# A convolution buffer of its own, and modulation chunks moved out of the output projection

## The chip, the cores and the metric

The kernel runs on one core of a Trainium2 chip. The metric is the device time of one execution in microseconds (us); the profiled execution also has a span, from its first to its last instruction. Engines are named as in the profile: PE is TensorE (matmuls), PEld its weight loads, DVE is VectorE, ACT is ScalarE, POOL is GpSimd, SP is SyncE, which only issues DMAs here.

## The reference

Two layers of a diffusion backbone over 512 latent tokens and a prefix of 256 context tokens, width 2048. Each layer makes three modulation vectors from a conditioning vector, runs one input projection that feeds four groups, and one output projection:

```python
for l in range(DEPTH):                       # DEPTH = 2
    need_ctx = l < DEPTH - 1
    shift, scale, gate       = split(silu(c)     @ w_mod[l] + b_mod[l], 3)
    shift_c, scale_c, gate_c = split(silu(c_ctx) @ w_mod[l] + b_mod[l], 3)
    hl = rmsnorm(x,  g_pre[l]) * (1 + scale)   + shift
    hc = rmsnorm(xc, g_pre[l]) * (1 + scale_c) + shift_c
    pl, pc = split_proj(hl @ w_in[l]), split_proj(hc @ w_in[l])
    oA = chunk_sgu(p[0], p[1]) * silu(p[2])                 # spatial gating (SGU)
    oB = diff_attention(p[3..5]) * silu(p[6])
    oC = rwkv_mixer(p[7..9]) * silu(p[10])                  # both directions, a recurrence
    oD = short_conv(p[11], p[12], p[13]) * silu(p[14])      # three taps, bg * conv(cg * xin)
    x  = x  + gate   * rmsnorm(concat(oA..oD) @ w_out[l], g_post[l])
    if need_ctx: xc = xc + gate_c * rmsnorm(the same for the context, g_post[l])
return x
```

All of it is float32. Layer 1 needs the context only as keys, values and recurrent state.

## The kernel before

Activations stand transposed: 128 features by 768 tokens (256 context, then 512 latent). A projection tile (`mtile`, lines 281 to 306) is 128 output features: four steps, each with one 256 KB weight load on SP (`wr`), a rounding to a high part on ACT (`wh`, L276), a low part on POOL or, in every fourth step, on DVE (`wl`, L277), and 12 matmuls of 512 columns (latent), with 12 more of 256 where the context is wanted. The result is in a bank of PSUM from the pool `mm`, which has three; a tile with context takes two.

The stages follow each other in each layer:

- **Recurrence** (`recurrence`): for each of four feature tiles (ft) a chain over six segments of 256 tokens. A pipeline (`rwkv_pipe`) interleaves three segments: features (`seg_pre`), a triangular inverse (`seg_inverse`) and the chain (`seg_chain`), and then `seg_y`, which writes the segment's output into `yacc`. When ft is done, `rwkv_merge` normalises `yacc`, adds `bacc`, gates it and stores it (L888), beside the first segment of the next ft. Projection tiles of later ft (`rkv_tile`, `gate_tiles`) are issued between segments and fill PE. Behind the recurrence stand the convolutions that share its pool: two in layer 0, four in layer 1. A convolution (`conv`) is four projection tiles: `x`, the product `zp`, three taps into `o`, a product and a gate, a store (L1118).
- **Groups** (`groups_phase`): four attention heads, two convolutions among them in layer 0, then four SGU heads.
- **Output** (`out_mid` in layer 0): 16 projection tiles m for the latent tokens (v = 0), their normalisation, residual and the next layer's input; then the same for the context (v = 1). `out_last` is that of layer 1.

Buffers: a tag of a pool with `bufs=1` is one buffer. In the recurrence the tag `x` serves a temporary at the start, `bacc` of ft 0 and 2, and the convolution's `x`; the tag `o` serves a temporary at the start, `yacc` of ft 0 and 2, and the convolution's `o`; `bacc` and `yacc` have tags of their own for ft 1 and 3.

Modulation: the vector products are done in chunks (jobs) of 512 outputs. `gemv_dve` loads 16 slices of `w_mod` and adds them up on DVE, for both vectors (L222; the first product of each sum on ACT, L220); `gemv_end` sums over partitions with matmuls and adds the bias (L250, L253). Twelve jobs stand in layer 0's groups and output: four gates of layer 0 and eight chunks for layer 1. Eight run one beside each attention and SGU head, and four beside the 16 output tiles of v = 0, there in halves of 256 columns. Their instructions have lower priority than what is written around them.

The program's order on each engine, and on SP's queue, is fixed when it is built: a scheduler places every instruction by priority (program order, unless `high_priority` raises it) as soon as its inputs and its buffers allow it. On the chip each queue runs in that order.

Of the kernel before, what the change touches and what calls it, by code (L numbers as in the profile page):

```python
# [9 lines left out]
F32 = mybir.dt.float32  # L10
F32R = mybir.dt.float32r
F16 = mybir.dt.float16
AF = mybir.ActivationFunctionType
# [6 lines left out]
NCTX = 256  # L20
NLAT = 512
T = NCTX + NLAT
KT = 16
# [15 lines left out]
PADW = 774  # L39
# [64 lines left out]
class Kernel:  # L104
# [661 lines left out]
    def seg_y(self, s):  # L766
        l, ft, st, seg, want_y = (s[k] for k in ("l", "ft", "st", "seg", "want_y"))
        GM, SV, UV, AR = (s[k] for k in ("GM", "SV", "UV", "AR"))
        nc, rp, ps = self.nc, self.rp, self.ps
        V, A = nc.vector, nc.scalar  # L770
        if want_y:
            yp = ps.tile([128, 4, 2, 64], F32, tag="ps", name=self.nm("yp"))
            two = lambda t: t.rearrange("p a t -> p (a t)")
            for c in range(4):
                nc.tensor.matmul(out=yp[:, c], lhsT=two(UV[:, c]), rhs=GM[:, c, 1], start=True, stop=False)
                nc.tensor.matmul(out=yp[:, c], lhsT=two(SV[:, c]), rhs=AR[:, c, :, 1, :], start=False, stop=True)
            if "yacc" not in st:
                st["yacc"] = rp.tile([128, PADW], F32, tag=("o", "yacc")[ft % 2], name=self.nm("yacc"))
            ycol = st["yacc"][:, seg * SEG:(seg + 1) * SEG].rearrange("p (c t) -> p c t", c=4)
            for h in range(2):  # L780
                hs = slice(64 * h, 64 * h + 64)
                if st.get(("y", seg)):
                    V.tensor_tensor(out=ycol[hs], in0=yp[hs, :, h, :], in1=ycol[hs], op=ALU.add)
                else:
                    A.copy(out=ycol[hs], in_=yp[hs, :, h, :])
            st["y", seg] = True
# [104 lines left out]
    def groups_phase(self, l):  # L891
        nc, tc = self.nc, self.tc
        with tc.tile_pool(name=self.nm("gr"), bufs=1, reuse_waits="tile") as gp, \
                tc.tile_pool(name=self.nm("gsp"), bufs=3, space=PSUM, reuse_waits="tile") as sp, \
                tc.tile_pool(name=self.nm("gpp"), bufs=2, space=PSUM, reuse_waits="tile") as pp:
            self.gp, self.sp, self.pp = gp, sp, pp
            self.cs = gp.tile([128, 2, NLAT], F32, tag="cs", name=self.nm("cs"))
            nc.sync.dma_start(out=self.cs, in_=self.a["rope"])
            self.rot = gp.tile([128, 128], F32, tag="rot", name=self.nm("rot"))
            nc.sync.dma_start(out=self.rot, in_=self.a["rot"])  # L900
            self.sgw = gp.tile([128, 4, 128], F32, tag="sgw", name=self.nm("sgw"))
            nc.sync.dma_start(out=self.sgw, in_=self.a["sgw"][l])
            self.sgb = gp.tile([128, 4, 128], F32, tag="sgb", name=self.nm("sgb"))
            nc.sync.dma_start(out=self.sgb, in_=self.a["sgb"][l:l + 1].to_broadcast([128, 4, 128]))
            jobs = [(0, j, (0, 1)) for j in range(8, 12)] + [(1, j, (0, 1)) for j in range(8)]
            if l > 0:
                jobs = [(1, j, (0,)) for j in range(8, 12)]
            else:
                self.jobs, jobs = jobs[8:], jobs[:8]

            open_jobs = []
            late = ({('a', 1): 2, ('a', 3): 3}, {})[l]

            def mod_jobs(n):
                for ll, j, acc in open_jobs:
                    self.gemv_end(ll, j, acc, pp, "pp")
                open_jobs.clear()
                for _ in range(min(n, len(jobs))):
                    ll, j, vecs = jobs.pop(0)
                    with tc.high_priority(offset=-1000):  # L920
                        open_jobs.append((ll, j, self.gemv_dve(ll, j, vecs, gp, "gw", 4, ("gacc0", "gacc1"))))
            for h in range(4):
                mod_jobs(1)
                self.attention(l, h)
                if ("a", h) in late:
                    self.conv(l, late["a", h])
            for h in range(4):
                mod_jobs(1)
                self.sgu(l, h)
                if ("s", h) in late:  # L930
                    self.conv(l, late["s", h])
            mod_jobs(0)
# [156 lines left out]
    def conv(self, l, f):  # L1089
        nc, gp = self.nc, self.gp  # L1090
        V, G, A = nc.vector, nc.gpsimd, nc.scalar
        ctx = l < DEPTH - 1
        cs = slice(0 if ctx else NCTX, T)
        segs = ([(0, 0, NCTX, 2)] if ctx else []) + [(1, NCTX, NLAT, 260)]
        cw = self.P(l, "conv").rearrange("p (k f) -> p k f", k=3)
        x = gp.tile([128, T], F32, tag="x", name=self.nm("x"))
        p = self.proj(l, 6336 + f * 128, ctx=ctx)
        self.evac(x[:, 0:NCTX], x[:, NCTX:T], p)
        zp = gp.tile([128, PADW], F32, tag="stg" if gp is self.rp else "cz", bufs=2, name=self.nm("zp"))
        for c in (0, 258, 772):  # L1100
            G.memset(zp[:, c:c + 2], 0.0)
        p = self.proj(l, 6848 + f * 128, ctx=ctx)
        for i, o0, n, po in segs:
            with self.tc.high_priority():
                V.tensor_tensor(out=zp[:, po:po + n], in0=p[i][:, 0:n], in1=x[:, o0:o0 + n], op=ALU.mult)
        o = gp.tile([128, T], F32, tag="o", name=self.nm("o"))
        for i, o0, n, po in segs:
            s = slice(o0, o0 + n)
            A.activation(out=o[:, s], in_=zp[:, po:po + n], func=AF.Copy, scale=cw[:, 1, f:f + 1])
            for k, d in ((0, -1), (2, 1)):  # L1110
                V.scalar_tensor_tensor(out=o[:, s], in0=zp[:, po + d:po + d + n], scalar=cw[:, k, f:f + 1],
                                       in1=o[:, s], op0=ALU.mult, op1=ALU.add)
        p = self.proj(l, 5824 + f * 128, ctx=ctx)
        for i, o0, n, po in segs:
            V.tensor_tensor(out=o[:, o0:o0 + n], in0=p[i][:, 0:n], in1=o[:, o0:o0 + n], op=ALU.mult)
        sg = self.gate2(gp, self.proj(l, 7360 + f * 128, ctx=ctx), "stg" if gp is self.rp else "cz", 2)
        V.scalar_tensor_tensor(out=o[:, cs], in0=o[:, cs], scalar=0.5, in1=sg[:, cs], op0=ALU.mult, op1=ALU.mult)
        nc.sync.dma_start(out=self.od[12 + f][:, cs], in_=o[:, cs])  # L1118
# [13 lines left out]
    def out_mid(self, l):  # L1132
        nc, tc = self.nc, self.tc
        V, A = nc.vector, nc.scalar
        self.hc, self.hl = ([], []), ([], [])
        with tc.tile_pool(name=self.nm("op"), bufs=2, reuse_waits="tile") as op, \
                tc.tile_pool(name=self.nm("ops"), bufs=1, space=PSUM, reuse_waits="tile") as ops:
            for v in (0, 1):
                n = (NLAT, NCTX)[v]
                ts = slice(NCTX, T) if v == 0 else slice(0, NCTX)  # L1140
                y = [op.tile([128, n], F32, tag=f"y{v}", bufs=KT, name=self.nm("y")) for _ in range(KT)]
                pre = [self.wload(self.a["w_out"][l, :, 0], 128, (1 + i) % 4) for i in range(4)]
                self.wraw = op, 4
                o = self.load_o(v)
                accs, open_jobs = [], []
                for m in range(KT):
                    if v == 0 and m % 4 == 1:
                        for job in open_jobs:
                            self.gemv_end(*job, ops, "rs")
                        open_jobs = []  # L1150
                        if self.jobs:
                            ll, j, vecs = self.jobs.pop(0)
                            with tc.high_priority(offset=-1000):
                                acc = self.gemv_dve(ll, j, vecs, op, "y1", KT, ("y1", "y1"), NCTX, KT)
                            open_jobs.append((ll, j, acc))
                    p = self.mtile(self.a["w_out"][l, :, m], 128, o if v else None, None if v else o, 1,
                                   pre=None if m else pre)[1 - v]
                    sq = op.tile([128, n], F32, tag=f"acc{m}{v}" if m < 2 else f"sq{v}", bufs=1, name=self.nm("sq"))
                    A.activation(out=sq, in_=p[:, 0:n], func=AF.Square)
                    A.copy(out=y[m], in_=p[:, 0:n])  # L1160
                    if m < 2:
                        accs.append(sq)
                    else:
                        V.tensor_tensor(out=accs[m % 2], in0=accs[m % 2], in1=sq, op=ALU.add)
                for job in open_jobs:
                    self.gemv_end(*job, ops, "rs")
                rs = self.rstd_bcast(op, ops, "rs", accs, n, f"rs{v}")
                acc2 = []
                for m in range(KT):
# [13 lines left out]
                rs = self.rstd_bcast(op, ops, "rs", acc2, n, f"rs{v}")  # L1183
# [109 lines left out]
```

## Time and profile before

| | us |
|---|---|
| median of three runs | 3751.13 (3750.08 to 3751.83) |
| the profiled execution | 3740.13 |
| its span | 3738.3 |
| PE busy | 3448.6 (92%) |
| DVE busy | 2303.8 (62%) |
| ACT busy | 1863.0 (50%) |
| POOL busy | 1364.5 (36%) |

Busy time is a sum over the whole span, and a matmul's end is modelled, so that PE at 92% says only that most of the span has matmuls in it. The stages have different limits, and the rows below are taken by stage.

### The profile page before, as it was taken

How to read it: one execution, taken by the hardware profiler on the slowest of the kernel's cores; microseconds unless marked ns; L12 is line 12 of the kernel's file. 1: busy time of each engine (PE TensorE's matmuls, PEld its weight loads, DVE VectorE, ACT ScalarE, POOL GpSimd, SP SyncE). 2: the span in 40 equal slices, each digit the busy share in tenths (PEclk: the TensorE clock that was granted, in tenths of full speed). 3: DMA queues.
4: the chain of work that ended last, by engine and by line, in shares of the span. 5: the costliest groups of instructions: out<-in, count | busy, mean ns of one | idle time of the engine just before them, and what ended most of it. 6: DMA issues, size and time to landing. Idle time of an engine off the chain costs nothing. (4 is left out here: it accounts for less than half of the span.)

```text
span 3738.3 us, 61946 instructions
## 1 busy us (share of the span) xinstructions
PE 3448.6 (92%) x22388; PEld 2811.2 (75%) x22388; DVE 2303.8 (62%) x4659; ACT 1863.0 (50%) x4131; POOL 1364.5 (36%) x1729
## 2 busy tenths in 40 slices
PE   7999999989999999999897899999778999999998
PEld 2477777767877888888676777777566787788798
DVE  5856777777386546463878734767667526643354
ACT  4466666766244344223324435767666524544454
POOL 2244444534222222222444433545334332322343
PEclk9999999989999999999999999999668999999999
DMA  8432222211343313344655433122011244423565
GB/s 306 183 116 65 59 66 67 60 48 38 104 130 96 112 51 95 112 139 134 201 156 184 123 115 89 56 69 60 28 29 46 60 133 132 139 71 85 166 188 179
DMA packets 239747, 400.90 MB, mean 107 GB/s; under 512 B 25936, under 2 KB 95568, under 8 KB 235344
## 3 DMA queue, kind: packets, MB, share of 16 engines
q1 hardware_dynamic: 232528, 386.45, 34.3%
q10 hardware_dynamic: 6912, 10.49, 0.8%
q8 instruction: 176, 2.88, 0.3%
q14 instruction: 131, 1.07, 0.1%
HBM read 363.28 MB, written 33.56 MB: 106 GB/s over the span
## 5 line engine op out<-in xcount | busy, mean ns | idle before, releaser
L306 PE MATMUL p<-h,wh 128*128 128x512 f32 (+3 forms) x8576 | 2160.1, 349 | 34.5 <-ACT y L1160 10.7
L306 PEld LDWEIGHTS p<-h,wh 128*128 128x128 f32 (+1 forms) x8576 | 1415.4, 190 | 236.1 <-ACT h L276 15.8
L306 PE MATMUL p<-h,wl 128*128 128x512 f32 (+2 forms) x4288 | 1344.5, 350 | 46.1 <-DVE wl L277 28.9
L277 POOL TENSOR_TENSOR wl<-wr,wh 128x512 fp32r<-128x512 f32 (+1 forms) x535 | 768.4, 1439 | 1501.7 <-ACT wh L276 1317.8
L276 ACT CAST wh<-wr 128x512 fp32r<-128x512 f32 (+1 forms) x756 | 465.8, 617 | 974.1 <-PE p L306 772.2
L306 PEld LDWEIGHTS p<-h,wl 128*128 128x128 f32 (+1 forms) x4288 | 748.4, 190 | 147.7 <-DVE wl L277 35.8
L222 DVE SCALAR_TENSOR_TENSOR acc<-gw,sil,acc 128x512 f32<-128x512 f32 (+1 forms) x636 | 458.5, 778 | 27.4 <-DMA gw<-in_w_mod 25.1
L277 DVE TENSOR_TENSOR wl<-wr,wh 128x512 fp32r<-128x512 f32 (+1 forms) x221 | 160.9, 728 | 218.6 <-ACT wh L276 216.8
L804 PEld LDWEIGHTS <-ib 128*128 128x128 f16 x2304 | 133.2, 103 | 138.1 <-issue 70.0
L839 ACT CAST ib<-xa 64x256 f16<-64x256 f32 x480 | 176.2, 367 | 18.0 <-PE xa L809 12.2
L829 DVE TENSOR_TENSOR T<-inv,c 128x256 f16<-128x256 f32 x240 | 98.9, 412 | 34.5 <-PE inv L804 31.4
L1001 DVE TENSOR_REDUCE sm<-s 128x1 f32<-128x256 f32 (+1 forms) x144 | 74.8, 538 | 73.5 <-PE s L999 72.3
L741 POOL TENSOR_SCALAR sp<-SV,pcs 64x64 f32<-64x64 f32 x160 | 80.8, 509 | 105.5 <-DVE SV L762 81.0
L652 POOL TENSOR_TENSOR bk<-t_tw,kr 64x256 f32<-64x256 f32 x96 | 92.9, 968 | 36.1 <-DVE kr L636 32.4
L745 PE MATMUL ch<-SV,GM 128*128 128x128 f32 x384 | 89.5, 317 | 17.5 <-DVE SV L762 10.1
L1008 ACT ACTIVATE e<-s,sm 128x256 f32<-128x256 f32 (+1 forms) x144 | 80.9, 569 | 41.6 <-DVE sm L1005 33.3
L706 PE MATMUL g<-AR,BK 128*128 128x256 f32 (+1 forms) x384 | 96.7, 391 | 3.9 <-DVE BK L658 1.9
L748 PE MATMUL ch<-zs,xb 128*128 128x64 f32 x384 | 81.3, 296 | 15.0 <-ACT zs L747 13.6
L748 PEld LDWEIGHTS ch<-zs,xb 128*128 128x128 f32 x384 | 65.7, 204 | 38.5 <-ACT zs L747 32.5
L753 PE MATMUL ch<-UV,BKT 128*128 128x128 f32 x352 | 85.6, 328 | 9.6 <-ACT UV L750 8.6
L762 DVE SCALAR_TENSOR_TENSOR SV<-ch,pcs,sp 64x64 f32<-64x64 f32 x256 | 72.1, 281 | 35.4 <-PE ch L753 28.2
L745 PEld LDWEIGHTS ch<-SV,GM 128*128 128x128 f32 x384 | 64.4, 204 | 37.6 <-issue 9.3
(270 smaller groups left out, 5022.0 us busy)
## 6 DMA issues: line engine op xcount, KB each, us to landing
wr<-in_w_in SPq DMA_DIRECT2D x484, 256.0 KB, 2.7
wr<-in_w_out SPq DMA_DIRECT2D x256, 256.0 KB, 2.9
gw<-in_w_mod SPq DMA_DIRECT2D x192, 256.0 KB, 3.0
gw<-in_w_mod SPq DMA_DIRECT2D x32, 1024.0 KB, 6.6
gw<-in_w_mod SPq DMA_DIRECT2D x128, 128.0 KB, 3.2
raw<-rkvd SPq DMA_DIRECT2D x96, 128.5 KB, 2.2
lz<-lzd SPq DMA_DIRECT2D x48, 256.0 KB, 3.1
os<-od SPq DMA_DIRECT2D x32, 256.0 KB, 3.2
```

What stands on the lines that cost most here:

```text
L222: self.nc.vector.scalar_tensor_tensor(out=acc, in0=w, scalar=s, in1=acc, op0=ALU.mult, op1=ALU.add)
L276: self.nc.scalar.copy(out=hi, in_=raw)
L277: eng.tensor_tensor(out=lo, in0=raw, in1=hi, op=ALU.subtract)
L306: nc.tensor.matmul(out=p[0:w, 0:n], lhsT=a[:, kk, :], rhs=x[b][k], start=(first and kk == 0 and i == 0), stop=(last and kk == 3 and i == 2))
L652: G.tensor_tensor(out=bk[hs, :, h, :], in0=c4(an)[hs], in1=kn[hs], op=ALU.mult)
L706: nc.tensor.matmul(out=g[:, c], lhsT=bkc(c2 + c), rhs=AR[:, c2 + c, :, 0:nk, :], start=True, stop=True)
L745: nc.tensor.matmul(out=chp[:, 0:128], lhsT=two(GM[:, c, 0]), rhs=two(SV[:, c]), start=True, stop=True)
L748: nc.tensor.matmul(out=chp[:, 128:192], lhsT=XT32[:, c, :], rhs=zs, start=True, stop=True)
L753: nc.tensor.matmul(out=chp[:, 192:320], lhsT=BKT[:, c, :], rhs=two(UV[:, c]), start=True, stop=True)
L804: nc.tensor.matmul(out=out[:, c, :], lhsT=lhsT[:, c, :], rhs=rhs(c), **kw(c))
L829: V.tensor_tensor(out=T1, in0=p1, in1=bt(self.lm(d, j)), op=ALU.mult)
L839: A.copy(out=half(XT, h), in_=aXT[hs])
```

## The change

Three things. In the recurrence every ft's `yacc` has one tag and buffer of its own, `yacc`; the convolutions there use the tag `o` for `x` and write `o` into the same buffer, so that they share nothing with `yacc` and `bacc`. The four modulation jobs beside the output tiles move to the SGU heads of layer 0, which get two jobs each, in whole slices of 512 columns. And the two ACT copies out of each output tile's PSUM get high priority.

```diff
@@ seg_y
-                st["yacc"] = rp.tile([128, PADW], F32, tag=("o", "yacc")[ft % 2], name=self.nm("yacc"))
+                st["yacc"] = rp.tile([128, PADW], F32, tag="yacc", name=self.nm("yacc"))
@@ groups_phase
-                self.jobs, jobs = jobs[8:], jobs[:8]
+                self.jobs = []
...
             for h in range(4):
-                mod_jobs(1)
+                mod_jobs(1 if l else 2)
                 self.sgu(l, h)
@@ conv
-        x = gp.tile([128, T], F32, tag="x", name=self.nm("x"))
+        own = gp is self.rp
+        x = gp.tile([128, PADW if own else T], F32, tag="o" if own else "x", name=self.nm("x"))
...
-        o = gp.tile([128, T], F32, tag="o", name=self.nm("o"))
+        o = x if own else gp.tile([128, T], F32, tag="o", name=self.nm("o"))
@@ out_mid
-                accs, open_jobs = [], []
+                accs = []
                 for m in range(KT):
-                    if v == 0 and m % 4 == 1:
-                        for job in open_jobs:
-                            self.gemv_end(*job, ops, "rs")
-                        open_jobs = []
-                        if self.jobs:
-                            ll, j, vecs = self.jobs.pop(0)
-                            with tc.high_priority(offset=-1000):
-                                acc = self.gemv_dve(ll, j, vecs, op, "y1", KT, ("y1", "y1"), NCTX, KT)
-                            open_jobs.append((ll, j, acc))
                     p = self.mtile(self.a["w_out"][l, :, m], 128, o if v else None, None if v else o, 1,
                                    pre=None if m else pre)[1 - v]
                     sq = op.tile([128, n], F32, tag=f"acc{m}{v}" if m < 2 else f"sq{v}", bufs=1, name=self.nm("sq"))
-                    A.activation(out=sq, in_=p[:, 0:n], func=AF.Square)
-                    A.copy(out=y[m], in_=p[:, 0:n])
+                    with tc.high_priority():
+                        A.activation(out=sq, in_=p[:, 0:n], func=AF.Square)
+                        A.copy(out=y[m], in_=p[:, 0:n])
...
-                for job in open_jobs:
-                    self.gemv_end(*job, ops, "rs")
```

## Rows read from the trace of the kernel before

**Rows 1.** Part 1 of the profile page: busy time by engine.
```profile
PE 3448.6 (92%) x22388; PEld 2811.2 (75%) x22388; DVE 2303.8 (62%) x4659; ACT 1863.0 (50%) x4131; POOL 1364.5 (36%) x1729
```

**Rows 2.** Stretches: length, busy PE PEld DVE ACT POOL, PE clock, DMA share, GB/s.
```profile
1000.00:1100.00 100.00, 95.12 (x530) 80.37 (x529) 76.58 (x116) 32.87 (x65) 33.64 (x22) 0.98 0.54 165
1500.00:1768.00 268.00, 258.78 (x1497) 225.49 (x1495) 132.48 (x258) 77.10 (x133) 58.60 (x42) 0.99 0.42 125
1768.00:1969.00 201.00, 177.29 (x786) 143.69 (x786) 146.15 (x284) 61.91 (x114) 96.59 (x48) 0.98 0.59 178
1800.00:1925.00 125.00, 103.74 (x456) 83.13 (x456) 120.17 (x238) 35.20 (x66) 68.14 (x27) 0.99 0.62 189
1969.00:2107.00 138.00, 111.28 (x785) 100.94 (x784) 114.97 (x131) 66.94 (x132) 69.63 (x49) 0.94 0.54 168
```

**Rows 3.** Stretches, projection matmuls (L306) alone: length, PE, PEld, clock, DMA, GB/s.
```profile
795.00:820.00 25.00, 0.00 (x0) 0.00 (x0) 0.58 0.08 22
820.00:964.00 144.00, 90.73 (x400) 61.27 (x401) 0.99 0.18 50
964.00:1009.00 45.00, 45.00 (x258) 39.13 (x257) 1.00 0.26 73
2610.00:2830.00 220.00, 0.00 (x0) 0.00 (x0) 0.67 0.09 26
2830.00:2985.00 155.00, 89.37 (x291) 50.58 (x292) 0.96 0.20 55
2985.00:3063.00 78.00, 78.00 (x346) 64.59 (x345) 1.00 0.37 105
```

**Rows 4.** Instructions in order of time, 2836 to 2842 us.
```profile
2837.95 0.72 POOL L884 TENSOR_TENSOR yacc<-yacc,bacc 128x256 f32<-128x256 f32 x1
2838.70 0.59 ACT L333 COPY x<-p 128x512 f32<-128x512 f32 x1 [0.75 <-POOL yacc L884]
...
2839.16 0.33 SPq L888 DMA_DIRECT2D od<-yacc  x1
```

**Rows 5.** Instructions in order of time: a write of `yacc`, and its stores.
```profile
471.32 0.75 ACT L785 COPY yacc<-yp 64x256 f32<-64x256 f32 x2 [0.65 <-PE yp L776]
...
475.68 0.32 SPq L888 DMA_DIRECT2D od<-yacc  x1
...
826.51 0.32 SPq L888 DMA_DIRECT2D od<-yacc  x1
...
2670.96 0.33 SPq L888 DMA_DIRECT2D od<-yacc  x1
...
2984.28 0.33 SPq L888 DMA_DIRECT2D od<-yacc  x1
```

**Rows 6.** One line of the kernel, L888: its DMAs from issue to landing.
```profile
DMA to landing us min/median/max: 2.0/2.3/3.3
```

**Rows 7.** Groups by form, 1500 to 1768 us: busy, mean ns, idle before.
```profile
L222 DVE SCALAR_TENSOR_TENSOR acc<-gw,sil,acc 128x512 f32<-128x512 f32 x90 | 74.0, 879 | 0.0
L277 POOL TENSOR_TENSOR wl<-wr,wh 128x512 fp32r<-128x512 f32 x42 | 58.6, 1395 | 207.7 <-ACT wh L276 207.7
```

**Rows 8.** Groups by form, 1768 to 1969 us.
```profile
L222 DVE SCALAR_TENSOR_TENSOR acc<-gw,sil,acc 128x256 f32<-128x256 f32 x240 | 123.2, 584 | 8.8 <-DMA gw<-in_w_mod 8.8
L277 POOL TENSOR_TENSOR wl<-wr,wh 128x512 fp32r<-128x512 f32 x48 | 97.0, 2028 | 112.5 <-ACT wh L276 104.1 <-DMA gw<-in_w_mod 8.4
L306 PE MATMUL p<-h,wl 128*128 128x512 f32 x241 | 96.3, 399 | 21.4 <-DVE wl L277 14.1 <-POOL wl L277 7.1
```

**Rows 9.** Waits: total us, times, longest; DVE's from 1500 to 1768.
```profile
DVE mod L253 <- PE gps L250: 53.0, 4, 13.4
```

**Rows 10.** Waits of PE from 1969 to 2107.
```profile
PE p L306 <- ACT y L1160: 10.7, 1, 10.7
```

**Rows 11.** Waits of SP's queue from 1500 to 2120.
```profile
SPq L236 <- DVE acc L222: 66.9, 98, 3.0
```

## The prediction

> **What bounds the kernel now.** I read busy time first [rows 1]: PE is the engine that sets the pace over the whole, so a change pays where PE stands idle or is out of work, and costs where it makes PE wait. Next come the stretches by stage [rows 2], and then the same with the projection matmuls alone [rows 3], because only these can be moved about; the rest of PE's work in the recurrence waits for its own chain. Two stretches of the recurrences hold no projection at all: 25 us in layer 0 (795 to 820) and 220 us in layer 1 (2610 to 2830). In the second PE's granted clock averages 0.67, so two thirds of it ran at the lower of the two levels. Right behind each recurrence stands the opposite: 45 us (964 to 1009) and 78 us (2985 to 3063) in which PE does projections alone. These are convolutions that came too late. What held them is seen in order of time [rows 4]: `x` of the first convolution is copied out of PSUM at the moment in which the merge of ft 2 has read `bacc` for the last time, at 2838.7. The buffer was the limit, not the priority.
>
> In the output stage [rows 2] PE is idle for 201 - 177.3 = 23.7 us of v = 0, where DVE is 96% busy from 1800 to 1925, and PE waits for low parts `wl` from DVE and POOL [rows 8]. Of v = 1 one wait of 10.7 us stands out, for a copy of ACT out of PSUM [rows 10].
>
> **The convolutions of layer 1.** They need no less work, but may now run from the start of the recurrence. The place for them is the empty 220 us. Beside the chain, the kernel before hosts 291 projection matmuls in the 155 us from 2830 on [rows 3], 1.88 per us. The empty stretch could so take 413; what is left over at 2985 is 346. All of it fits, by a margin of 67. The recurrence itself should not get longer: a feature tile takes (826.51 - 475.68) / 2 = 175 us in layer 0 with PE full, the empty one in layer 1 takes 2839.16 - 2670.96 = 168, and the last one, with convolutions beside it, 145 [rows 4, 5]. So the stage ends with the last merge at 2984.3, not with the last convolution at 3063: at most 79 us. I take 75, for a small hole at the turn to the groups; if hosting is a fifth slower (330 matmuls), 16 stay behind, and with a slower chain 60 is my lower bound.
>
> At full PE the higher clock comes back too, but the row of 168 us against 175 says that the chain gains nothing from it, so I count it as zero. The Trainium skill (TensorE: Matmul & The Clock Gate, Terms) prices time at a lowered clock at that time times the share of pulses withheld; that would give a further gain, which is a rival below. No run here has yet shown the chain faster for it.
>
> **The convolutions of layer 0.** The empty 25 us take 25 x 400 / 144 = 69 matmuls, and at the end 258 of them took 45 us: 12 us. PE is nearly full before that, so I expect little more. Bounds: 0, and 25 if the narrow gaps ahead of 795 are filled as well.
>
> **One buffer for `x` and `o`.** The next convolution's `x` now waits for the store of the one before, 2.0 to 3.3 us by the same kind of store [rows 6]; two projection tiles can meanwhile fill PSUM, so I count nothing. Without that cover it would be 3 us for each of four.
>
> **One `yacc`.** The first write of the next ft must now wait for the merge's store to land. In layer 0 the write stands at 471.3 and the store at 475.7 [rows 5], landing some 2.3 us later [rows 6]: 7 us, three times. In layer 1 the first written segment comes two segments later, so nothing waits. Late with it is one of two PSUM buffers that `seg_pre` and `seg_scores` share; these are two segments ahead of the chain, and the end of the stage is set by what convolutions remain. I take 2, between 0 and 21.
>
> **The output stage.** Removed from v = 0: 240 DVE instructions, 123.2 us [rows 8], 128 loads of SP's queue, 32 matmuls, and 8 first products of ACT. DVE keeps 146.2 - 123.2 = 23 us of work in 201. I take the whole idle time of PE less a little for the start: 24 counting the seams between matmuls. Bounds: 14 (the wait for `wl` is partly due to ACT) and 30. The v = 1 part cannot hide it, since its start is tied to v = 0's PSUM and DVE.
>
> **The copies.** High priority puts them ahead of the normalisation's ACT work; the 10.7 us [rows 10] may go whole, or not at all where DVE, 83% busy there [rows 2], is next. I take 6. A copy at the head of ACT's queue holds the next roundings `wh` until its tile ends, but those are three steps ahead: nothing.
>
> **SGU.** Added: 120 DVE products. At 879 ns [rows 7] that is 105 us, so DVE goes from 132.5 to 238 of 268 us, 89%. Also 64 loads of 256 KB, 16.8 MB or 63 GB/s more on 125, which is less than 1800 to 1925 moves [rows 2]. They stand in SP's queue ahead of weight loads, and SP has waited 66.9 us over 98 such loads, 3.0 at most [rows 11]; the weights have three buffers, so this alone costs little. Eight first products go to ACT, which is 29% busy. The 32 small matmuls move too. What a DVE at 89% costs PE I read between two rows [rows 2]: 4.9% of idle time at 76.6%, 17% at 96%; linearly 12.6%, against 3.4% now, so 25 us. But SGU tiles have 768 columns where the output has 512, so each `wl` has half as much time again; the nearer row, 1000 to 1100 with such tiles, would give 4. I take 16. Bounds 0 and 40: the second is this 25 and a slip of the last two jobs into the output stage.
>
> A rule speaks against this place: the Trainium skill (SBUF — State Buffer, SBUF: two separate sides) says that a DVE instruction with two inputs in SBUF and a GpSimd instruction that reads SBUF shut each other out for their whole length. The rows lean that way: POOL's `wl` takes 2028 ns beside the products in the output stage and 1395 in the SGU stretch [rows 7, 8]. Taken literally, 238 of DVE and 58.6 of POOL would need 297 us in turn, 29 more than the 268 there are, and the sum would be 3665.
>
> **Sum.** -75 -12 +2 -24 -6 +16 = -99 us. The profiled execution took 3740.1, 11 less than the median of the runs shown; I put the same 99 on the median: 3751.1 - 99 = 3652 us.
>
> **Rivals.**
>
> 1. *DVE becomes the bound beside SGU.* For it: 89%, and DVE also stands still there 53.0 us for the small matmuls of `gemv_end` [rows 9], which if kept make 238 + 53 = 291 of 268. With the slip above +40 in place of +16: 3676. Against: these waits shrink when DVE arrives later.
>
> 2. *The convolutions stay late*, because the scheduler puts them, last in program order, behind another shortage (PSUM banks, the staging buffers they share with `rkv_tile`). Then only the output stage and SGU count: -30 + 16 + 2 = -12, 3739. Against: rows 4 show `x` copied within 0.1 us of its buffer's release.
>
> 3. *The clock is worth more than I grant.* If the chain ran at the lower level for 66% of 220 us, 145 us, and half of that came back, 73 more: 3579. Against: 168 us for the empty tile.
>
> 4. *Slower: convolutions admitted early hold banks that the chain's own projections need.* A convolution tile in layer 0 takes two of three `mm` banks for 96 matmuls, at 400 in 144 us [rows 3] 35 us. `rkv_tile` is issued three segments (175 / 6 x 3 = 88 us) ahead, so only waits over 88 us cost. The change loses when the chain is held for over 99 us in all, 33 at each of layer 0's three turns of ft: 121 us of waiting, 3.5 convolution tiles ahead of one `rkv_tile`. With four ahead (140 us), 52 at each turn, 156 in all: 3808. For it: only eight such tiles exist, but they are ready from the start. Against: lower priority.
>
> **How the numbers follow.** Likeliest, as summed: 66%, own range 3630 to 3670. Rival 1: 18%. Rival 2: 8%. Rival 3: 3%. Rival 4: 5%. The bounds together reach from 3751 - 79 - 25 - 30 - 11 = 3606 to 3751 - 60 - 14 + 40 + 21 = 3738; not all fall on one side, and the range that leaves out two in ten is 3615 to 3702, which holds the likeliest case and rival 1. A change of 0.2% (7.5 us) is about what a measurement of this kernel can tell from none. Faster: 66 + 18 + 3, and most of rival 2, 93%; within 0.2%: 2%; slower: 5%.
>
> **What would show it.** Right: projection matmuls all through what is now 2610 to 2830, a clock near 1.0 there, the rope load of layer 1's groups some 2 us behind the last store of `yacc`, no L222 in the output stage, PE idle there under 5 us in v = 0, and `wl` on POOL back near 1395 ns. In SGU: PE idle near 25 us of 280, DVE near 89%. Wrong: an empty stretch that remains, recurrences that take over 180 us for a feature tile (rival 4), SGU heads that are 10 us longer each or products that run on into the output stage (rival 1).

## The result, and the profile after

The changed kernel takes 3628.25 us (median of four runs, 3628.01 to 3636.34), the kernel before in the same session 3750.61. The ratio is 0.968, 95% interval 0.966 to 0.970. The medians are 122 us apart, and by the ratio it is 119 us less, where the prediction said 99 less and 3652, range 3615 to 3702. The profiled executions have spans of 3738.3 and 3626.4, 111.9 apart; the account by stage below is made with these two.

First, part 1 of the page of the changed kernel, busy time by engine.

```profile
PE 3401.8 (94%) x22388; PEld 2756.9 (76%) x22388; DVE 2295.1 (63%) x4539; ACT 1858.4 (51%) x4123; POOL 1340.3 (37%) x1729
```

PE has the same 22388 matmuls as in [rows 1]. DVE has lost 120 instructions (240 halves became 120 whole slices) and only 9 us; ACT has lost 8, as 16 first products in halves became 8 whole ones (the prediction counted 8 in v = 0, where there were 16).

Now the projection matmuls (L306) alone, in the stretches that were empty and in the tail of layer 1's recurrence (columns as in [rows 3]).

```profile
795.00:820.00 25.00, 15.12 (x65) 9.93 (x65) 1.00 0.12 33
2610.00:2830.00 220.00, 130.88 (x415) 70.44 (x415) 1.00 0.26 73
2830.00:2964.00 134.00, 83.27 (x289) 47.49 (x289) 0.99 0.19 53
```

Both empty stretches are full, at the rates that the prediction read off their neighbours: 65 matmuls where it said 69, and 415 where it said 413. The granted clock there is 1.00, where [rows 3] have 0.58 and 0.67. Next the end of that recurrence on SP's queue: the last store of `yacc`, a weight load, and the rope table with which the groups begin.

```profile
2963.93 0.33 SPq L888 DMA_DIRECT2D od<-yacc  x1
2965.84 0.33 SPq L281 DMA_DIRECT2D wr<-in_w_in  x1
2966.22 0.42 SPq L898 DMA_DIRECT2D cs<-in_rope  x1
```

The groups begin 2.3 us behind the chain, and no convolution stands between. The stretches of layer 0's SGU heads, of the output's v = 0 and of v = 1 (columns as in [rows 2]) come from both kernels, cut at the same instructions: from the last attention store to the last SGU product, and at the copies of the first and the last output tile of each kind. Before:

```profile
1498.20:1763.60 265.40, 256.99 (x1492) 224.46 (x1491) 130.24 (x253) 76.22 (x131) 58.60 (x42) 0.99 0.42 124
1773.80:1968.40 194.60, 173.34 (x774) 141.07 (x772) 144.73 (x281) 58.26 (x108) 93.84 (x47) 0.99 0.58 175
1968.40:2106.60 138.20, 111.48 (x789) 101.34 (x789) 114.75 (x130) 67.14 (x132) 69.83 (x49) 0.94 0.54 168
```

After:

```profile
1488.20:1774.30 286.10, 269.57 (x1544) 234.16 (x1544) 216.63 (x369) 77.31 (x127) 62.85 (x42) 0.97 0.56 169
1785.80:1954.50 168.70, 167.44 (x723) 137.59 (x724) 35.74 (x41) 57.81 (x107) 60.99 (x48) 0.98 0.37 109
1954.50:2088.00 133.50, 112.28 (x779) 102.31 (x778) 115.85 (x126) 66.94 (x132) 74.17 (x49) 0.94 0.55 173
```

SGU is 20.7 us longer, v = 0 is 25.9 shorter, v = 1 is 4.7 shorter. In v = 0 the reader sees what a stage looks like whose bound has gone: DVE falls from 145 to 36 us, POOL from 94 to 61 for the same low parts, and PE stands idle for 1.3 us instead of 21.3.

The account, in us of the profiled spans (negative is a gain), from differences of such marks. Each row counts from the mark before it: layer 1's recurrence from the copy of the last output tile (2106.6, now 2088.0), the first attention head from the rope load to the issue of the head's store (112.3 us, now 97.3).

| stage | predicted | measured |
|---|---|---|
| recurrence and convolutions, layer 0 (rope load at 1011.6, now 1001.5) | -12 + 2 | -10.1 |
| SGU heads, layer 0 | +16 | +20.7 |
| start of the output, between the last SGU product and the first tile's copy | in the above | +1.3 |
| output, v = 0 | -24 | -25.9 |
| output, v = 1 | -6 | -4.7 |
| recurrence and convolutions, layer 1 (rope load at 3065.1, now 2966.2) | -75 | -80.3 |
| first attention head of layer 1 | 0 | -15.0 |
| all else | 0 | +2.1 |

### The profile page after: what moved, and what is told of

It reads as the page before. It is cut to its first block, busy times and chain, and to the rows that moved or that the text cites. A ratio compares the mean times of both kernels' runs of the same rounds, so it can differ in the third digit from the quotient of the medians.

```text
span 3626.4 us, 61613 instructions
## 1 busy us (share of the span) xinstructions
PE 3401.8 (94%) x22388; PEld 2756.9 (76%) x22388; DVE 2295.1 (63%) x4539; ACT 1858.4 (51%) x4123; POOL 1340.3 (37%) x1729
## 5 line engine op out<-in xcount | busy, mean ns | idle before, releaser
L306 PE MATMUL p<-h,wh 128*128 128x512 f32 (+3 forms) x8576 | 2194.4, 352 | 36.6 <-ACT x L331 10.5
L306 PEld LDWEIGHTS p<-h,wh 128*128 128x128 f32 (+1 forms) x8576 | 1421.2, 191 | 234.7 <-ACT x L331 14.1
L306 PE MATMUL p<-h,wl 128*128 128x512 f32 (+2 forms) x4288 | 1353.2, 352 | 27.0 <-DVE wl L277 18.7
L277 POOL TENSOR_TENSOR wl<-wr,wh 128x512 fp32r<-128x512 f32 (+1 forms) x535 | 743.2, 1391 | 1456.5 <-ACT wh L276 1285.4
L306 PEld LDWEIGHTS p<-h,wl 128*128 128x128 f32 (+1 forms) x4288 | 752.3, 191 | 123.5 <-DVE wl L277 22.9
L222 DVE SCALAR_TENSOR_TENSOR acc<-gw,sil,acc 128x512 f32<-128x512 f32 x516 | 432.7, 888 | 19.3 <-DMA gw<-in_w_mod 15.8
L277 DVE TENSOR_TENSOR wl<-wr,wh 128x512 fp32r<-128x512 f32 (+1 forms) x221 | 157.1, 711 | 203.0 <-ACT wh L276 199.1
L804 PEld LDWEIGHTS <-ib 128*128 128x128 f16 x2304 | 118.6, 99 | 123.9 <-issue 66.9
L1157 DVE TENSOR_TENSOR sq<-sq,sq 128x512 f32<-128x512 f32 (+1 forms) x28 | 28.8, 1028 | 111.6 <-ACT sq L1152 111.6
L835 ACT CAST X<-xa 128x256 f16<-128x256 f32 x192 | 71.3, 372 | 44.8 <-PE xa L809 41.9
L745 PE MATMUL ch<-SV,GM 128*128 128x128 f32 x384 | 82.9, 298 | 10.2 <-DVE SV L762 4.8
L646 DVE TENSOR_TENSOR AR<-kr,Pt 64x512 f32<-64x512 f32 (+1 forms) x96 | 89.8, 935 | 2.8 <-ACT Pt L621 0.8
```

What stands on the lines that cost most here:

```text
L222: self.nc.vector.scalar_tensor_tensor(out=acc, in0=w, scalar=s, in1=acc, op0=ALU.mult, op1=ALU.add)
L277: eng.tensor_tensor(out=lo, in0=raw, in1=hi, op=ALU.subtract)
L306: nc.tensor.matmul(out=p[0:w, 0:n], lhsT=a[:, kk, :], rhs=x[b][k], start=(first and kk == 0 and i == 0), stop=(last and kk == 3 and i == 2))
L646: V.tensor_tensor(out=AR[hs, :, h, 0:nk, :], in0=kr[hs, :, 0:nk, :], in1=Pva[hs, :, 0:nk, :], op=ALU.mult)
L745: nc.tensor.matmul(out=chp[:, 0:128], lhsT=two(GM[:, c, 0]), rhs=two(SV[:, c]), start=True, stop=True)
L804: nc.tensor.matmul(out=out[:, c, :], lhsT=lhsT[:, c, :], rhs=rhs(c), **kw(c))
```

## Experiments

All ratios are to the kernel before, run beside it on the same chip, with 95% intervals.

**The buffers alone (e1_conv_only).** The diff of `seg_y` and `conv`, without the other two parts.

> Only the buffers of the recurrence change (one yacc, x and o of the convolution in one buffer); the modulation jobs and the copies stay as in the kernel before. My theory: the convolutions carry nearly all of the gain, 10 us in layer 0, 79 us in layer 1 and some 15 us at layer 1's first attention head, whose projections PE can take while the chain ends: ratio 0.972, some 3646 us. Rival (the moved modulation jobs and the copies carry a third or more of the gain): above 3670 us.

Measured: 3643.81 us, 0.973 (0.971 to 0.974). The buffers carry most of the gain: the medians are 100 us apart. In its profile layer 1's groups begin at 2976.5, again 2.3 us behind the last store of `yacc`.

**The modulation jobs alone (e2_mod_only).** Buffers and copies as before:

```diff
-                self.jobs, jobs = jobs[8:], jobs[:8]
+                self.jobs = []
...
-                mod_jobs(1)
+                mod_jobs(1 if l else 2)
                 self.sgu(l, h)
```

> Only the four modulation jobs move from the output tiles to the SGU heads. My theory: each SGU head gets 6 to 7 us longer and the start of the output 5, some 22 us in all, and the 16 output tiles of v = 0 get 26 us shorter: nearly nothing is left, 3743 to 3750 us. Rival (the gain of the output stage is the larger by far, the SGU cost came from something else in the change): 3725 to 3735 us.

Measured: 3735.02 us, 0.9975 (0.9965 to 0.9985), 6 to 13 us less by the interval. The kernel before took 3744.04 beside it, not 3751; as a difference, 9 us came where I had expected 1 to 8. The stretch of SGU heads took 287.1 us and v = 0 169.0 in its profile, against 265.4 and 194.6 before: the move gives with one hand what it takes with the other, and a small gain is left.

**The copies alone (e3_copies_only).** Only `with tc.high_priority():` around the two ACT instructions.

> Only the two ACT copies out of each output tile get high priority. My theory: the wait of 10.7 us in v = 1 goes, and some 5 us of it reach the end: 3744 to 3748 us. Rival (DVE is next, nothing reaches the end): 3751 us.

Measured: 3741.03 us, 0.9993 (0.9984 to 1.0002): at most 6 us, and no change is not excluded. PE's waits in v = 1 of this kernel (total, times, longest):

```profile
PE p L306 <- DVE wl L277: 8.9, 9, 2.0
PE p L306 <- POOL wl L277: 7.9, 9, 1.2
PE p L306 <- ACT wh L276: 3.9, 4, 1.3
```

The wait for the copy [rows 10] is gone, and what remains is mainly waits for low parts.

**One yacc alone (e4_yacc_only).** The first line of the diff only; the convolution's `x` still shares its buffer with `bacc`.

> Only yacc gets one buffer for all feature tiles; the convolution's x stays with bacc. If the wait for the merge's store is what makes a feature tile of layer 0 take 182 us instead of 175 after the change, it does so here too, and the whole is 7 to 15 us slower, 3758 to 3766 us, with layer 1's chain as before. Rival (the convolutions beside the chain make it longer): a feature tile takes 175 us here, and the whole stays at 3751 us.

Measured: 3757.18 us, 1.0028 (1.0019 to 1.0037), slower by 7 to 14 us. Two stores of `yacc` in layer 0, a feature tile apart:

```profile
656.56 0.32 SPq L888 DMA_DIRECT2D od<-yacc  x1
...
840.95 0.32 SPq L888 DMA_DIRECT2D od<-yacc  x1
```

That is 184 us, and the feature tile before it took 182, where [rows 5] have 175 on average. Without convolutions to fill PE the shared buffer's wait reaches the end of the run: the groups of layer 0 begin at 1026.9 instead of 1011.6. The order of copy and store is seen in the changed kernel:

```profile
474.92 0.32 SPq L888 DMA_DIRECT2D od<-yacc  x1
478.07 0.75 ACT L785 COPY yacc<-yp 64x256 f32<-64x256 f32 x2
```

In [rows 5] the copy stood at 471.3, ahead of the store. Now it follows the store by 3.1 us and stands 6.8 us later than it did.

**yacc in three buffers (e7_yacc_by_segment).** The changed kernel, with the same memory cut by segment, each stored when merged:

```diff
-                st["yacc"] = rp.tile([128, PADW], F32, tag="yacc", name=self.nm("yacc"))
+                ys[seg] = rp.tile([128, SEG], F32, tag=f"yacc{seg}", name=self.nm("yacc"))
...
-        nc.sync.dma_start(out=self.od[8 + ft][:, lo:T], in_=y[:, lo:T])
+            nc.sync.dma_start(out=self.od[8 + ft][:, s], in_=y)
```

> The changed kernel with yacc as three buffers of 256 columns, each stored when its segment is merged, in the same memory. The next feature tile's first write then waits only for the first segment's merge. My theory: a feature tile of layer 0 goes from 182 us back to 175, the chain ends some 14 us earlier, and the stage, which still has convolutions to do, 5 to 12: 0.2 to 0.3% faster than the changed kernel. Rival (the wait is hidden, PE is full anyway): the stage of layer 0 ends at 1001 us as it does now.

Measured: 3627.71 us, 0.968 (0.966 to 0.970). SP's queue in layer 0: three last stores of feature tiles, and the rope load of the groups.

```profile
479.60 0.32 SPq L887 DMA_DIRECT2D od<-yacc  x1
...
829.51 0.32 SPq L887 DMA_DIRECT2D od<-yacc  x1
...
964.42 0.32 SPq L887 DMA_DIRECT2D od<-yacc  x1
...
1001.93 0.42 SPq L898 DMA_DIRECT2D cs<-in_rope  x1
```

A feature tile is back at 175 us and the chain ends at 964 instead of 978. The groups begin at 1001.9, as in the changed kernel (1001.5). My expectation of 5 to 12 us was wrong and the rival right: with convolutions beside the chain, PE's own work sets the end of this stage. From the chain's end to the rope load PE is busy without a gap, all of it projections: 37.5 of 37.5 us here, 23.3 of 23.3 in the changed kernel.

**Half of the products (e6_fewer_products).** The changed kernel with one condition in `gemv_dve`:

```diff
                 for v in vecs:
-                    self.gemv_acc(acc[v, c], w, k, v, k == 0)
+                    if not (l == 1 and 4 <= j < 8 and k >= 8):
+                        self.gemv_acc(acc[v, c], w, k, v, k == 0)
```

> The changed kernel without the second half of the products (slices 8 to 15) of the four moved jobs; their loads all stay. This leaves part of layer 1's scale out. If DVE's load makes the SGU heads longer, they go from 65 us to some 60, and the whole gets 10 to 15 us faster. Rival (SP's queue and the 64 loads make it): heads stay at 64 us or more and the time stays.

Measured: 3614.51 us, 0.9655 (0.9634 to 0.9676). By the ratios that is some 10 us under the changed kernel, as expected, but the two intervals overlap, so the reading goes by the stretch. The SGU stretch of this kernel:

```profile
1491.10:1765.10 274.00, 267.58 (x1548) 233.12 (x1547) 174.77 (x321) 79.88 (x135) 61.24 (x42) 0.98 0.58 179
```

274.0 us against 286.1 with all products and 265.4 before; PE is idle for 6.4 us, against 16.5 and 8.4. All 64 loads are still there (179 GB/s), so DVE's products make the added idle time, not the loads. What remains of the cost, 8.6 us, is in PE's own busy time, which is 10.6 us above before. Most of that is the small matmuls of `gemv_end`, 32 of which moved here: they took 17.9 us of PE in this stretch, against 9.2 before.

**Jobs beside attention (e5_mod_attention).** The changed kernel with

```diff
-                mod_jobs(1)
+                mod_jobs(1 if l else (2, 2, 2, 1)[h])
                 self.attention(l, h)
...
-                mod_jobs(1 if l else 2)
+                mod_jobs(1 if l else (2, 1, 1, 1)[h])
                 self.sgu(l, h)
```

> The changed kernel, but three of the four moved modulation jobs stand beside attention heads: two jobs beside heads 0, 1 and 2 and beside SGU head 0, one beside the others. My theory: the SGU cost of 22 us comes from DVE, which has to take six jobs without a pause from 1578 to 1779; attention heads are 100 us and more and pay little. SGU heads go back to 58 us, attention pays under 5, ratio to before 0.963 to 0.965, some 15 us faster than the changed kernel. Rival (the loads, not DVE's place, cost it; or attention pays as much): within 5 us of the changed kernel.

Measured: 3626.75 us, 0.968 (0.966 to 0.970), no different from the changed kernel. The SGU stretch fell from 286 to 262 us in its profile, and the attention heads took it back. The second attention head of the changed kernel, then of this one:

```profile
1134.70:1230.10 95.40, 91.11 (x534) 77.74 (x533) 66.45 (x129) 44.01 (x95) 21.27 (x15) 0.98 0.32 94
```

```profile
1133.70:1246.50 112.80, 103.44 (x585) 88.03 (x584) 88.87 (x163) 46.11 (x98) 27.65 (x17) 0.96 0.40 120
```

One more job, 17 us more. The next stretch, with a convolution, also took one job more (60 products for 32) and got 2.3 us shorter, and the last attention head, again with one more, 14.0 us longer. So the theory that the SGU heads are an especially bad place fell with this run.

**Both of these (e8_both).** e7's buffers with e5's order of jobs.

> Both of these together, as the best version: the gains add up, some 25 us faster than the changed kernel, ratio to before near 0.961. Rival: an earlier end of the recurrence only makes another stage wait, and no more than the larger of the two gains remains.

Measured: 3630.27 us, 0.969 (0.967 to 0.971). Nothing adds up, because neither part had a gain to add.

**Jobs beside convolutions (e9_mod_beside_convs).** The same two lines with other numbers:

```diff
+                mod_jobs(1 if l else (1, 2, 1, 2)[h])
...
+                mod_jobs(1 if l else (2, 1, 2, 1)[h])
```

> The changed kernel with the twelve jobs in another order: one, two, one, two beside the attention heads and two, one, two, one beside the SGU heads, so that two run at a time only at the first head, beside the two convolutions of the groups, and in one SGU head. My theory: a second job costs PE 6 to 17 us where the head's own chain goes through DVE in short steps and nothing else is there for PE, and nothing where a convolution's projections fill the gaps (the attention head with a convolution took 161.6 us with one job and 159.3 with two): some 12 us faster than the changed kernel. Rival (a job costs its 6 us wherever it stands): the same as the changed kernel.

Measured: 3620.68 us, 0.9677 (0.9663 to 0.9690). It is the lowest median but for the run that leaves products out; yet its interval overlaps that of the changed kernel run beside it, so a gain isn't shown. The attention head with a convolution took 166.6 us here with two jobs, where the changed kernel's took 161.6 with one: not free, as I had thought from e5, where it took 159.3.

**The changed kernel again (e10_changed_again).**

> The changed kernel itself, as the measure for the run beside it: ratio to before between 0.966 and 0.970.

Measured: 3628.91 us, 0.969 (0.967 to 0.971).

## Why the prediction was right

The time lay within its range and on its side, and the main mechanism, the convolutions' buffer, is the one that was named. The size is in part luck: of the profiled gain 15.0 us come from a step that the sum did not have, and the SGU cost that it set too low takes some of this back. Point by point:

- *The convolutions of layer 1* were held by `bacc`'s buffer, and once free they fill the empty stretch at the predicted rate. Shown by the matmul counts and by e1. The term was 75 and came out at 80.3; the hole that I had allowed for is not there. What the sum lacked is the step after it. I ended the account at the start of the groups, but the last convolution's store is issued at 2923, 41 us ahead of the chain's end, so PE could go on to projections of layer 1's first attention head, whose results then wait in PSUM. ACT's copies of q, k and v out of PSUM in the kernel before, and then in the changed one:

```profile
3071.97 0.58 ACT L333 COPY x<-p 128x512 f32<-128x512 f32 x1
...
3089.81 0.59 ACT L333 COPY x<-p 128x512 f32<-128x512 f32 x1
...
3107.82 0.59 ACT L333 COPY x<-p 128x512 f32<-128x512 f32 x1
```

```profile
2964.36 0.58 ACT L333 COPY x<-p 128x512 f32<-128x512 f32 x1
...
2977.78 0.59 ACT L333 COPY x<-p 128x512 f32<-128x512 f32 x1
...
2989.91 0.59 ACT L333 COPY x<-p 128x512 f32<-128x512 f32 x1
```

  They came 18 us apart, the time of a projection with context; now the first comes 0.4 us behind the issue of the chain's last store of `yacc` (2963.93), and the others 12 to 13 apart. So the first head ends 15.0 us earlier. e1, without the other parts, shows it too: the store of its first head follows its rope load by 98.8 us, where that took 112.3 before. That this head gains because of the projections held ready is read from these times; no run took it away by itself.
- *The clock* (rival 3) did not shorten the sum. In the changed kernel the feature tile that had no projections beside it runs at 1.00 and takes 172 us, against 168 at 0.68. Below are that tile before, the same tile now (columns as in [rows 2]), and the projection matmuls in it now (columns as in [rows 3]).

```profile
2670.96:2839.16 168.20, 125.51 (x970) 101.70 (x970) 114.83 (x287) 107.89 (x275) 60.51 (x130) 0.68 0.10 28
2655.45:2827.42 171.97, 161.90 (x1286) 121.81 (x1286) 133.86 (x304) 124.95 (x305) 89.86 (x156) 1.00 0.25 71
2655.45:2827.42 171.97, 100.20 (x312) 52.74 (x312) 1.00 0.25 71
```

  The chain's own matmuls took 125.5 us of PE before and take some 162 - 100 = 62 now, an estimate from these lines; those of L745 and L753 went from means of 398 and 422 ns to 298 and 295. So they got shorter at the higher clock, while 100 us of projections came between them. That the tile's time hardly moved shows only that the two together gain nothing. The prediction's row, 168 against 175, mixed the same two things and compared tiles of different layers: its zero was right for the sum, but its reason, that the chain gains nothing from the clock, is not shown. No run has the chain alone at the full clock, so the price that the Trainium skill puts on a lowered clock (TensorE: Matmul & The Clock Gate, Terms) is neither borne out nor refuted here.
- *The convolutions of layer 0 and one yacc*: -10.1 against -12 + 2. The wait of some 7 us per turn is shown by e4, and by e7 that it costs this stage nothing when convolutions cover it; so the convolutions gave 10 where 12 were counted, and `yacc` took nothing where 2 were. *One buffer for `x` and `o`* was put at nothing; in layer 1 the last convolution is stored 41 us ahead of the chain's end, so no wait there reached the end.
- *The output stage*: -25.9 against -24, with no L222 left there and `wl` on POOL at 1293 ns instead of 2028 [rows 8]. The 24 were to be idle time of PE; 20.0 us of the gain are that, and the other 5.9 are busy time, about what the moved small matmuls had taken there (6.5 us). *The copies*: the wait went, and -4.7 against -6 in v = 1; on the whole time e3 can't tell it from nothing.
- *SGU*: +20.7 (and 1.3 at the start of the output) against +16. The mechanism, a loaded DVE that makes PE wait, is right only in part: idle time of PE grew by 8.1 us, where 16 were counted, and DVE was busy for 76% of the stretch, not 89%. The other 12.6 us are longer busy time of PE. The mis-sized step is "The 32 small matmuls move too", to which I gave no price on PE, and beside it a slower clock that the sum did not have. The small matmuls of `gemv_end` took 15.1 us there instead of 9.2, and the projection matmuls, as many as before (1344 and 1340), 249.9 instead of 242.0, at a granted clock of 0.97 instead of 0.99. PE's longest waits of the stretch are these, and before it only the first was there, with 5.6 us:

```profile
PE mx L1077 <- DVE vn L1069: 6.9, 3, 2.4
PE p L306 <- DVE o L1084: 6.8, 3, 2.6
```

  Both are for steps of the heads themselves on DVE, which share its queue with the products. With half of the products (e6) they are 2.2 and 1.6 us. The Trainium skill's rule of the shared port (SBUF — State Buffer, SBUF: two separate sides), taken literally, gave 29. That sum did not set the size: measured, DVE and POOL come to 216.6 + 62.9 = 279.5 us of the 286.1, and PE waits nowhere in the stretch for POOL's `wl`, although this is slowed from 1395 [rows 7] to 1507 ns (`L277`, 40 of them from 1500 to 1785). Whether two single instructions shut each other out is not decided by these sums.
- *Rival 2* did not come: all convolutions moved. *Rival 4* did not either, although its sign did, a feature tile over 180 us in layer 0 (182). The sign was badly chosen, as the 7 us that the prediction counts for `yacc` make 182 of 175 without the rival. e4 has the longer tile without the early convolutions, and e7 has these and 175 us. *Rival 1* came in part: products run from 1578 to 1779, the last five behind the last SGU product, for 22 us in all and not 40.

What stays open: why the moved jobs cost about as much in one place as in another. Single stretches pay very unequally for one job more (17.4, -2.3 and 14.0 us in e5, 5.0 in e9, 22.0 for four in the SGU heads), and yet the times of the changed kernel, e5 and e9 can't be told apart. In the SGU heads part of it is traced to steps of DVE behind the products; in the attention heads no run separates the causes.

## What to carry to other kernels

When an engine is idle in one stretch and does only movable work right behind it, look at which buffer the first instruction of that work waited for: here the release and the start lay 0.03 us apart. The rate of the neighbouring stretch told here how much of the work the empty one would take, 413 matmuls where 415 came. Follow such a gain past the next stage's first instruction, because freed time pulls work across the border. Filler on an engine that others wait for is not free just because that engine's average load is low: here, moving it from one stage to the next mostly moved its cost.

## What I had not expected of the hardware

The mean of POOL's low part hides two things. A `wl` of 128x512 took 1293 ns where no products ran (v = 0 of the changed kernel, DVE busy for 21%), 1507 on average beside 512-column products and 2028 beside 256-column ones. But the last mean is made by a few: its smallest, median and largest are, in the output stage of the kernel before,

```profile
L277 POOL TENSOR_TENSOR wl<-wr,wh x48: 1275/1438/7815, 1771.1 to 1968.1; 128x512 fp32r<-128x512 f32 x48
```

while the median in the SGU stretch of the changed kernel is 1512 and the longest 2232. One that took 6.92 us, from 1809.65 on, lay inside a row of 21 products that DVE ran in 8.40 us from 1806.44:

```profile
1806.44 8.40 DVE L222 SCALAR_TENSOR_TENSOR acc<-gw,sil,acc 128x256 f32<-128x256 f32 x21
1809.65 6.92 POOL L277 TENSOR_TENSOR wl<-wr,wh 128x512 fp32r<-128x512 f32 x1 [4.41 <-ACT wh L276]
```

Each of the 21 took 472 to 480 ns, so POOL was held up and DVE was not. It does not always come out so: 21 products from 1790.17 on took 11.52 us, beside three `wl` of 1.31 to 1.46 us. No run shows what decides.
